# The RG-LRU is computed as a whole beside its gate products; small reciprocal roots become a power on GpSimd

## The chip, the cores and the metric

The kernel runs on one NeuronCore of a Trainium2 chip. The number that counts is the device time of one execution in microseconds (us). Beside it stands one profiled execution, whose span runs from its first to its last instruction.

## The reference

Two layers of a diffusion backbone run over 256 context tokens and 512 latent tokens (T = 768 columns), with a model width of 1024. In each layer one input projection feeds three branches, each 512 channels wide: differential attention, a bidirectional gated recurrence (RG-LRU) and a bidirectional gated DeltaNet. Their outputs are merged by gates, projected and followed by an MLP. The branch that is changed is this, cut to its core:

```python
r = sigmoid(x @ gate_w[d, 0] + gate_b[d, 0])       # per direction d, x after a width-4 convolution
i = sigmoid(x @ gate_w[d, 1] + gate_b[d, 1])
log_a = -LRU_C * r * softplus(-lam[d])
a = exp(log_a)
b = sqrt(-expm1(2 * log_a)) * (i * x)
h_t = a_t * h_(t-1) + b_t                          # context first, then latent; d = 1 backwards
out = gelu(y) * (h of d=0 + h of d=1)
```

The reciprocal roots belong to the RMS norms and the l2 norms, `rsqrt(mean(x*x) + EPS)`. The second layer computes no context outputs, so there most of the work is 512 columns wide, while keys, values and the states of both recurrences still need the context.

## The kernel before, in words

**Matrix products.** Each fp32 product is made of three products of rounded parts. A weight unit `raw` (512 KB) is loaded by SP's DMA queue, ScalarE rounds it to `wh` and VectorE makes the rest `wl` (`split`, L176). The pools `raw`, `wts` (`wh`) and `wtl` (`wl`) hold three units each. `mm_feat` (L203) multiplies: for each of 8 input blocks `wh` with the high part, `wh` with the low part, `wl` with the high part.

**Recurrence and fill.** `gdn_core` ends in a recurrence of 24 steps (`pgd` tiles, L725 to L829), each step a chain TensorE, ScalarE, TensorE, VectorE, TensorE, ScalarE. Behind it in the program stand the "fill" projections, which do not need its result: gates of the merge (`fill_gate`, `pgt`), the RG-LRU's input (`fill_lx`, `plx`) and its gate products (`fill_lx_gates`, `plg`), the gelu input (`fill_ly`, `py`), the DeltaNet's output gate (`fill_gz`, `pz`), queries, keys and values (`pqk`, `pv`). A scheduler orders all instructions when the program is built. It takes the ready instruction that stands first in the program, except inside `tc.high_priority()`, which moves evictions and weight loads ahead. So the fill goes into the recurrence's gaps. Once built, each engine runs its own list strictly in order.

**Buffers.** An instruction that first writes a tile is ready only if the pool has a free buffer. Two pools matter here: `t3` (six buffers of 776 columns) holds nearly all intermediate tiles of the fill, and `big` holds two PSUM tiles, which every fill product needs one of. A PSUM tile is free again when ScalarE has evicted it into a `t3` tile. One `t3` buffer is held by the tile `rope` of `da_tables` (L1047): its second use (L1055, L1058, for the queries' tables) writes tiles with the tags `gcol` and `geb`, and these buffers belong to `R.col` and `R.ge`, which the recurrence reads to its last step.

**RG-LRU.** It has 4 channel blocks j and 2 directions d. Inside the fill, `fill_lx_gates` makes the four gate products of a block, evicts each as `lsg` (L924) and stores it to DRAM (`lrs`). After the recurrence `lru` (L1003 to L1031) loads them into `slab` tiles (`lW`) and does the rest: Exp, Tanh and Square on ScalarE, a VectorE product, Sqrt, products with the gated input, three scans on VectorE, a sum on GpSimd and the product with the stored gelu value `lys`. It runs at the same time as `gdn_out` and the attention's key preparation (`da_load`, `da_keys`, with `dkx` and `pdt`). On ScalarE, Sqrt and the pair Exp/Tanh need different function tables (ACT_TABLE_LOAD).

**Small roots.** `rsqrt` (L130) is called 23 times on 128 x 2 to 128 x 48 values: Sqrt on ScalarE, reciprocal and a Newton step on VectorE.

Of the kernel before, what the change touches and what calls it, by code (L numbers as in the profile page):

```python
# [48 lines left out]
def hybrid_prefix_dit_block_kernel(  # L49
# [68 lines left out]
    epsc = cp.tile([P, 1], F32, name="epsc")  # L118
    G.memset(epsc, EPS)
# [118 lines left out]
    lrs = [dp.tile([P, 4, T], F32, name=f"lrs{i}") for i in range(4)]  # L238
# [192 lines left out]
    def norm(xT, L, gcol, sh, sc, name, parts, sq):  # L431
# [5 lines left out]
        for v, o, m in parts:  # L437
            nt = m // P
            with tc.high_priority():
# [6 lines left out]
                rsqrt(r6[:, 0:nt], v6[:, 0:nt], nt, ps[:, 0:nt], 1.0 / D)  # L446
# [460 lines left out]
    def fill_lx_gates(l, L, j, y, weights):  # L907
# [3 lines left out]
        for a0, a1, o, src in parts:  # L911
            S.copy(yh[:, a0:a1], src)
            G.tensor_tensor(yl[:, a0:a1], src, yh[:, a0:a1].bitcast(F32), op=OP.subtract)
        for d in range(2):
            for g in range(2):
                ps = big("plg")
                i = 2 * d + g
                for n, (w, x) in enumerate(((wh, yh), (wh, yl), (wl, yh))):
# [78 lines left out]
    def lru(l, L, full, mark):  # L997
        last = [None]
        t0 = 0 if full else TC
        lh = slab("lh").rearrange("p (k t) -> p k t", k=4)  # L1000

        def act(*args, **kw):
            i = S.activation(*args, **kw)  # L1003
            if last[0] is not None:
                behind(i, last[0])
            last[0] = i

        for j in range(4):
            W = []
# [492 lines left out]
```

## Time and profile before

| | |
|---|---|
| median of 3 runs | 2781.7 us (2779.94 to 2784.17) |
| profiled execution, its own time | 2784.37 us |
| its span | 2782.6 us |
| TensorE busy | 2652.2 us, 95% of the span |
| VectorE, ScalarE, GpSimd busy | 54%, 40%, 18% |
| mean granted TensorE clock | 0.973 |

Busy times are sums over the instructions of an engine. TensorE instructions are pipelined and their ends are modelled, so a TensorE that is shown busy can still be slowed by its clock: 1.00 is 2.4 GHz, 0.50 is 1.2 GHz, and values between them are means over a stretch. What a stage costs is read from that stage.

### The profile page before, as it was taken

The page shows a single profiled execution, that of the slowest core. Times are in us where ns is not written, and L with a number is a line of the kernel's source. Part 1 is how long each engine was busy: PE and PEld are TensorE (multiplying, and loading weights), DVE is VectorE, ACT ScalarE, POOL GpSimd, SP SyncE. Part 2 cuts the span into 40 slices and gives each one's busy share as a digit, 9 for nine tenths or more (in the row PEclk, how much of TensorE's full clock was granted, in tenths as well). Part 3 has the DMA queues.
Part 4 walks back from the last instruction along what each step waited for, and adds up shares of the span by engine and source line. Part 5 has one row for each costly group of instructions (what it writes and reads, how often), then busy time and mean ns, then how long its engine had stood idle before and what let it go on. Part 6 is the DMA issues. An engine that isn't in the chain of part 4 may idle for free. (4 is left out here: it accounts for less than half of the span.)

```text
span 2782.6 us, 44426 instructions
## 1 busy us (share of the span) xinstructions
PE 2652.2 (95%) x17741; PEld 2261.6 (81%) x17741; DVE 1496.1 (54%) x2520; ACT 1105.4 (40%) x2042; POOL 487.6 (18%) x638
## 2 busy tenths in 40 slices
PE   8999999998999989999999989999998698999999
PEld 5788888987888777888888887887997587888887
DVE  6658553557376543333333476786437776544344
ACT  4242454357366233221222243345437655432321
POOL 3001221214112122110101120032222311211100
PEclk9989999998999999999999999999999699999999
DMA  8433232245433643333332222334225343333332
GB/s 274 138 88 94 83 104 99 78 145 160 150 99 101 205 132 114 121 104 118 121 114 76 85 76 75 105 111 145 81 70 180 138 125 103 99 105 97 93 99 76
DMA packets 315589, 318.67 MB, mean 115 GB/s; under 512 B 19500, under 2 KB 268408, under 8 KB 314488
## 3 DMA queue, kind: packets, MB, share of 16 engines
q1 hardware_dynamic: 315384, 315.84, 36.1%
q8 instruction: 140, 2.29, 0.4%
q14 instruction: 65, 0.53, 0.1%
HBM read 259.70 MB, written 56.10 MB: 113 GB/s over the span
## 5 line engine op out<-in xcount | busy, mean ns | idle before, releaser
L176 ACT CAST wh<-raw 128x1024 fp32r<-128x1024 f32 x288 | 302.2, 1049 | 935.4 <-PE pm L203 614.1
L176 DVE TENSOR_TENSOR wl<-raw,wh 128x1024 fp32r<-128x1024 f32 x288 | 365.0, 1267 | 450.0 <-ACT wh L176 441.1
L203 PE MATMUL pm<-hdh,wh 128*128 128x256 f32 (+1 forms) x896 | 297.4, 332 | 0.5
L203 PE MATMUL pm<-hdl,wh 128*128 128x256 f32 (+1 forms) x896 | 294.5, 329 | 0.0
L203 PE MATMUL pm<-hdh,wl 128*128 128x256 f32 (+1 forms) x896 | 294.3, 328 | 0.0
L1325 DVE SCALAR_TENSOR_TENSOR xT<-pm,mod,xT 128x256 f32<-128x256 f32 (+1 forms) x224 | 133.8, 597 | 235.8 <-PE pm L203 235.8
L203 PE MATMUL pm<-hml,wh 128*128 128x512 f32 (+1 forms) x800 | 243.7, 354 | 5.8 <-DVE hml L461 5.8
L203 PE MATMUL pm<-hmh,wh 128*128 128x512 f32 (+1 forms) x800 | 242.4, 352 | 4.1 <-ACT mr L1306 2.8
L203 PE MATMUL pm<-hmh,wl 128*128 128x512 f32 (+1 forms) x800 | 240.3, 349 | 0.0
L1308 POOL TENSOR_TENSOR mq<-mr 128x768 f32<-128x768 f32 (+1 forms) x64 | 106.5, 1664 | 692.6 <-ACT mr L1306 684.3
L203 PEld LDWEIGHTS pm<-hdh,wh 128*128 128x128 f32 x896 | 170.1, 190 | 30.2 <-DVE xT L1325 8.4
L203 PE MATMUL pgt<-hnh,wh 128*128 128x512 f32 x576 | 181.0, 368 | 10.4 <-ACT gty L873 10.4
L203 PEld LDWEIGHTS pm<-hdh,wl 128*128 128x128 f32 x896 | 170.1, 190 | 15.2
L203 PEld LDWEIGHTS pm<-hdl,wh 128*128 128x128 f32 x896 | 170.2, 190 | 14.7
L203 PE MATMUL pgt<-hnh,wl 128*128 128x512 f32 x576 | 181.9, 365 | 0.0
L203 PE MATMUL pgt<-hnl,wh 128*128 128x512 f32 x576 | 178.1, 364 | 0.0
L203 PEld LDWEIGHTS pm<-hmh,wh 128*128 128x128 f32 x800 | 134.5, 190 | 32.4 <-ACT mr L1306 6.5
L203 PEld LDWEIGHTS pm<-hml,wh 128*128 128x128 f32 x800 | 135.4, 190 | 25.8 <-DVE hml L461 6.7
L203 PEld LDWEIGHTS pm<-hmh,wl 128*128 128x128 f32 x800 | 136.0, 191 | 21.7
L203 PEld LDWEIGHTS pgt<-hnh,wh 128*128 128x128 f32 x576 | 98.4, 194 | 27.7 <-ACT gty L873 12.0
L203 PEld LDWEIGHTS pgt<-hnh,wl 128*128 128x128 f32 x576 | 98.4, 193 | 16.8
L203 PEld LDWEIGHTS pgt<-hnl,wh 128*128 128x128 f32 x576 | 98.2, 195 | 16.7
(431 smaller groups left out, 6058.4 us busy)
## 6 DMA issues: line engine op xcount, KB each, us to landing
raw<-in_mlp_w_dram SPq DMA_DIRECT2D x128, 512.0 KB, 4.0
raw<-in_w_in_dram SPq DMA_DIRECT2D x120, 512.0 KB, 4.1
raw<-in_ada_w_dram SPq DMA_DIRECT2D x80, 512.0 KB, 4.2
lrs<-lsg SPq DMA_DIRECT2D x32, 384.0 KB, 2.3
lW<-lrs SPq DMA_DIRECT2D x16, 768.0 KB, 4.7
raw<-in_w_branch_dram SPq DMA_DIRECT2D x24, 512.0 KB, 3.9
gts<-gty SPq DMA_DIRECT2D x24, 384.0 KB, 4.8
mgg<-gts SPq DMA_DIRECT2D x24, 384.0 KB, 4.2
```

What stands on the lines that cost most here:

```text
L176: return S.copy(hi, src), V.tensor_tensor(lo, src, hi.bitcast(F32), op=OP.subtract)
L203: last = PE.matmul(ps[:, o:o + n], lhsT=w, rhs=r[:, t0:t0 + n], start=(k == 0 and i == 0), stop=(k == nk - 1 and i == 2))
L1308: G.tensor_tensor(q[:, 0:nt], r[:, 0:nt], r[:, 0:nt], op=OP.mult)
L1325: V.scalar_tensor_tensor(xv, ps[:, 0:m], L.mod[:, 40 + n, v:v + 1], xv, op0=OP.mult, op1=OP.add)
```

## The change

`fill_lx_gates` and the long `lru` are gone. `fill_lru` takes their place in the fill: all of the RG-LRU of a block is done from its gate products to the sum of both directions, in `t3` tiles, with no store or load between. Its tiles are the input `ly`, per direction the gate `lsg` that becomes the root, the decay `lat`, the square `lu`, and a second `lsg` (the input gate, which becomes h). `fill_ly` follows it and multiplies the gelu value with that sum; one result is stored per block (`lys`), and `lru` only loads it. The blocks now run as lx, gz, lru, ly each. `rsqrt` has no Sqrt and no reciprocal: GpSimd raises the value to the power -0.5.

```diff
-    def rsqrt(dst, v, n, src=None, scale=1.0):
-
-        w = mp.tile([P, 3, 48], F32, name="rsq", tag="rsq")
-        s, r, u = (w[:, i, 0:n] for i in range(3))
-        if src is None:
-            S.activation(s, v, AF.Sqrt)
-        else:
-            S.activation(s, src, AF.Sqrt, scale=scale, bias=epsc)
-        V.reciprocal(r, s)
+    def rsqrt(dst, v, n):
+
+        w = mp.tile([P, 2, 48], F32, name="rsq", tag="rsq")
+        r, u = (w[:, i, 0:n] for i in range(2))
+        G.tensor_tensor(r, v, bc(mhalf, [P, n]), op=OP.pow)
         V.scalar_tensor_tensor(u, r, -0.5, r, op0=OP.mult, op1=OP.mult)
...
-    def fill_lx_gates(l, L, j, y, weights):
+    def fill_lru(l, L, full, j, y, weights):
+
+        t0 = 0 if full else TC
         wh, wl = weights
         yh, yl = (gp.tile([P, T], F32R, name="gy", tag="g") for _ in range(2))
         parts = ((0, TC, 512, y[:, 0:TC]), (TC, T, 0, y[:, 259:771]))
         for a0, a1, o, src in parts:
             S.copy(yh[:, a0:a1], src)
             G.tensor_tensor(yl[:, a0:a1], src, yh[:, a0:a1].bitcast(F32), op=OP.subtract)
+
+        def gate(i):
+            ps = big("plg")
+            for n, (w, x) in enumerate(((wh, yh), (wh, yl), (wl, yh))):
+                for a0, a1, o, src in parts:
+                    PE.matmul(ps[:, o:o + a1 - a0], lhsT=w[:, i, :], rhs=x[:, a0:a1], start=(n == 0), stop=(n == 2))
+            r = t3("lsg")[:, 0:T]
+            for a0, a1, o, src in parts:
+                with tc.high_priority():
+                    S.activation(r[:, a0:a1], ps[:, o:o + a1 - a0], AF.Tanh, scale=0.5,
+                                 bias=L.gb[:, 4 * i + j:4 * i + j + 1])
+            return r
+
+        decay, root = [], []
         for d in range(2):
-            for g in range(2):
-                ps = big("plg")
-                i = 2 * d + g
-                for n, (w, x) in enumerate(((wh, yh), (wh, yl), (wl, yh))):
-                    for a0, a1, o, src in parts:
-                        PE.matmul(ps[:, o:o + a1 - a0], lhsT=w[:, i, :], rhs=x[:, a0:a1], start=(n == 0), stop=(n == 2))
-                r = t3("lsg")
-                for a0, a1, o, src in parts:
-                    with tc.high_priority():
-                        S.activation(r[:, a0:a1], ps[:, o:o + a1 - a0], AF.Tanh, scale=0.5,
-                                     bias=L.gb[:, 8 * d + 4 * g + j:8 * d + 4 * g + j + 1])
-                    if g == 1:
-                        V.scalar_tensor_tensor(r[:, a0:a1], r[:, a0:a1], 1.0, src, op0=OP.add, op1=OP.mult)
-                nc.sync.dma_start(lrs[j][:, 2 * d + g, :], r[:, 0:T])
-
-    def fill_ly(l, L, a, full, j):
+            r = gate(2 * d)
+            at, u = t3("lat")[:, 0:T], t3("lu")[:, 0:T]
+            c = slice(4 * d + j, 4 * d + j + 1)
+            S.activation(at, r, AF.Exp, scale=L.s8[:, c], bias=L.s8[:, c])
+            S.activation(r, r, AF.Tanh, scale=L.ns8[:, c], bias=L.ns8[:, c])
+            S.activation(u, at, AF.Square)
+            V.scalar_tensor_tensor(r, u, 1.0, r, op0=OP.add, op1=OP.mult)
+            decay.append(at)
+            root.append(r)
+        i = S.activation(root[0], root[0], AF.Sqrt)
+        behind(S.activation(root[1], root[1], AF.Sqrt), i)
+        hs = []
+        for d, (at, r) in enumerate(zip(decay, root)):
+            h = gate(2 * d + 1)
+            for a0, a1, o, src in parts:
+                V.scalar_tensor_tensor(h[:, a0:a1], h[:, a0:a1], 1.0, src, op0=OP.add, op1=OP.mult)
+            (V if d else G).tensor_tensor(r, r, h, op=OP.mult)
+            if d == 0:
+                V.tensor_tensor_scan(h, at, r, 0.0, op0=OP.mult, op1=OP.add)
+            else:
+                V.tensor_tensor_scan(h[:, TC - 1::-1], at[:, TC - 1::-1], r[:, TC - 1::-1], 0.0, op0=OP.mult, op1=OP.add)
+                V.tensor_tensor_scan(h[:, T - 1:TC - 1:-1], at[:, T - 1:TC - 1:-1], r[:, T - 1:TC - 1:-1], h[:, 0:1],
+                                     op0=OP.mult, op1=OP.add)
+            hs.append(h)
+        G.tensor_tensor(hs[0][:, t0:T], hs[0][:, t0:T], hs[1][:, t0:T], op=OP.add)
+        return hs[0]
+
+    def fill_ly(l, L, a, full, j, hs):
...
+        V.scalar_tensor_tensor(y[:, 0:nt], y[:, 0:nt], 0.25, hs[:, t0:T], op0=OP.mult, op1=OP.mult)
...
-        last = [None]
+    def lru(full, mark):
         t0 = 0 if full else TC
         lh = slab("lh").rearrange("p (k t) -> p k t", k=4)
-
-        def act(*args, **kw):
-            i = S.activation(*args, **kw)
-            if last[0] is not None:
-                behind(i, last[0])
-            last[0] = i
-
         for j in range(4):
-            W = []
-            for d in range(2):
-                W.append(slab("lW").rearrange("p (k t) -> p k t", k=4))
-                after(nc.sync.dma_start(W[d][:, 0:2, :], lrs[j][:, 2 * d:2 * d + 2, :]), mark)
-            r, ix, at, u = ([W[d][:, i, :] for d in range(2)] for i in range(4))
-            for d in range(2):
-                c = slice(4 * d + j, 4 * d + j + 1)
-                act(at[d], r[d], AF.Exp, scale=L.s8[:, c], bias=L.s8[:, c])
-                act(r[d], r[d], AF.Tanh, scale=L.ns8[:, c], bias=L.ns8[:, c])
-                act(u[d], at[d], AF.Square)
-                V.scalar_tensor_tensor(r[d], u[d], 1.0, r[d], op0=OP.add, op1=OP.mult)
-            for d in range(2):
-                act(r[d], r[d], AF.Sqrt)
-                (V if d else G).tensor_tensor(r[d], r[d], ix[d], op=OP.mult)
-            yl = ix[1]
-            nc.sync.dma_start(yl[:, t0:T], lys[j][:, t0:T])
-            hs, a1, b1, u1 = lh[:, j, :], at[1], r[1], u[1]
-            V.tensor_tensor_scan(hs, at[0], r[0], 0.0, op0=OP.mult, op1=OP.add)
-            V.tensor_tensor_scan(u1[:, TC - 1::-1], a1[:, TC - 1::-1], b1[:, TC - 1::-1], 0.0, op0=OP.mult, op1=OP.add)
-            V.tensor_tensor_scan(u1[:, T - 1:TC - 1:-1], a1[:, T - 1:TC - 1:-1], b1[:, T - 1:TC - 1:-1], u1[:, 0:1],
-                                 op0=OP.mult, op1=OP.add)
-            G.tensor_tensor(hs[:, t0:T], hs[:, t0:T], u1[:, t0:T], op=OP.add)
-            V.scalar_tensor_tensor(hs[:, t0:T], yl[:, t0:T], 0.25, hs[:, t0:T], op0=OP.mult, op1=OP.mult)
+            after(nc.sync.dma_start(lh[:, j, t0:T], lys[j][:, t0:T]), mark)
         return lh
...
-        y = fill_lx(l, L, a, full, 0)
         for j in range(4):
             gw = lx_gate_weights(l, j)
-            fill_ly(l, L, a, full, j)
-            yn = fill_lx(l, L, a, full, j + 1) if j < 3 else None
-            fill_lx_gates(l, L, j, y, gw)
-            y = yn
-        for j in range(4):
+            y = fill_lx(l, L, a, full, j)
             fill_gz(l, L, a, full, j)
+            hs = fill_lru(l, L, full, j, y, gw)
+            fill_ly(l, L, a, full, j, hs)
```

How the built programs stand, at three places. In the changed program the line numbers are shifted by a few: its L785 to L824 is the recurrence, L199 the fill products, L916 the gate products.

First, TensorE in layer 0, from step 4 of the recurrence on. Before: the step's products, then fill rows (`plx`) ahead of the next piece of the chain.

```order
L798 MATMUL pgd<-gB,gW 32x128 x4
L798 MATMUL pgd<-gB,gQT 32x128 x4
L798 MATMUL pgd<-gA,gW 32x128 x4
L798 MATMUL pgd<-gA,gQT 32x128 x4
L760 MATMUL pgd_1936<-gW 128x128 x2
L203 MATMUL plx<-hnl,wh 128x512
L203 MATMUL plx<-hnl,wh 128x256
L203 MATMUL plx<-hnh,wl 128x512
L203 MATMUL plx<-hnh,wl 128x256
L203 MATMUL plx<-hnh,wh 128x512
L203 MATMUL plx<-hnh,wh 128x256
L203 MATMUL plx<-hnl,wh 128x512
```

Now, from the same step on, behind the last row of the fourth gate product of block 0:

```order
L916 MATMUL plg<-gy,gwl 128x512
L793 MATMUL pgd<-gB,gW 32x128 x4
L793 MATMUL pgd<-gB,gQT 32x128 x4
L793 MATMUL pgd<-gA,gW 32x128 x4
L793 MATMUL pgd<-gA,gQT 32x128 x4
L755 MATMUL pgd_1929<-gW 128x128 x2
L813 MATMUL pgd_1929<-gW,gA 128x128
L813 MATMUL pgd<-gW,gA 128x128
L813 MATMUL pgd<-gW,gB 128x128
L813 MATMUL pgd_1929<-gW,gB 128x128
L813 MATMUL pgd<-gW,gA 128x128 x2
L813 MATMUL pgd<-gW,gB 128x128 x2
```

The fill has moved out. Before, 272 pairs of fill products (512 and 256 columns, same weights) and 653 further ones of 256 columns stand between step 4's products and step 23's; now none does. From step 4 to its end the recurrence is 590 rows of `pgd` in one piece, and `py`, the three later blocks, `pqk` and `pv` follow it. In layer 1 it is 578 rows in one piece, from step 2 on; before, 90 such pairs, 168 rows of 512 columns and 720 of 256 stood between step 2's products and step 23's.

Second, ScalarE at the end of the recurrence of layer 0 (L748, L806, L811 are the recurrence's copies; now L743, L801, L806). Before:

```order
L748 COPY gW<-pgd 128x128 x2
L806 COPY gW<-pgd 128x128
L811 ACTIVATE gA<-pgd,gcol 128x128
L806 COPY gW<-pgd 128x128
L811 ACTIVATE gB<-pgd,gcol 128x128
L965 COPY draw<-pqk 128x512
L966 ACTIVATE dsq<-pqk 128x512
L844 ACTIVATE osq<-gO 128x512 x2
L176 CAST wh<-raw 128x1024
L1003 ACTIVATE lW<-lW,s_3986 128x768
```

Now:

```order
L743 COPY gW<-pgd 128x128 x2
L801 COPY gW<-pgd 128x128
L806 ACTIVATE gA<-pgd,gcol 128x128
L801 COPY gW<-pgd 128x128
L806 ACTIVATE gB<-pgd,gcol 128x128
L931 ACTIVATE lu<-lat 128x768
L920 ACTIVATE lsg<-plg,cols 128x256
L920 ACTIVATE lsg<-plg,cols 128x512
L936 ACT_TABLE_LOAD
L936 ACTIVATE lsg<-lsg 128x768
```

The Square of the second direction of block 0 (`lu`) and the eviction of its third gate product stand behind the last step of the recurrence, although their inputs stand some 20 steps ahead of it. The buffers say why: `ly`, two `lsg`, two `lat` and `rope` are six `t3` tiles, and `rope` is let go only at the end of the recurrence. The third and fourth gate product hold both `big` tiles meanwhile.

Third, ScalarE within a block after the recurrence (block 1 of layer 0), against the gate evictions of a block before. Before:

```order
L924 ACTIVATE lsg<-plg,cols 128x256
L924 ACTIVATE lsg<-plg,cols 128x512
L912 CAST gy<-ly 128x256
L912 CAST gy<-ly 128x512
L729 ACTIVATE gW<-gVt,gcol 128x128 x2
L731 ACTIVATE gW<-gKt,gcol 128x128
L748 COPY gW<-pgd 128x128 x2
L731 ACTIVATE gW<-gKt,gcol 128x128
L176 CAST gwh<-gw 128x512
L937 COPY lyy<-py 128x768
L938 ACTIVATE lyq<-py 128x768
```

Now:

```order
L929 ACTIVATE lat<-lsg,s_3979 128x768
L930 ACTIVATE lsg<-lsg,ns_3980 128x768
L931 ACTIVATE lu<-lat 128x768
L920 ACTIVATE lsg<-plg,cols 128x256
L920 ACTIVATE lsg<-plg,cols 128x512
L929 ACTIVATE lat<-lsg,s_3979 128x768
L935 ACT_TABLE_LOAD
L935 ACTIVATE lsg<-lsg 128x768
L172 CAST wh<-raw 128x1024
L930 ACT_TABLE_LOAD
L930 ACTIVATE lsg<-lsg,ns_3980 128x768
L931 ACTIVATE lu<-lat 128x768
```

Between the eviction of the first gate product and that of the third (the first row below this piece) now stand two Exp, two Tanh, two Squares, a Sqrt, two table loads and a weight rounding. On TensorE the order in a block is `plx`, `pz`, 24 rows of `plg`, `py`, then `plx` of the next block.

## Rows read from the trace of the kernel before

**Rows 1.** Busy time by stage: from:to, length, PE, PEld, DVE, ACT, POOL, PEclk, DMA, GB/s.

```profile
328.70:589.30 260.60, 253.97 (x2353) 222.86 (x2341) 128.67 (x312) 114.38 (x292) 65.94 (x123) 0.99 0.31 99
1864.00:2111.80 247.80, 239.68 (x2214) 207.70 (x2216) 126.24 (x310) 111.16 (x293) 60.75 (x121) 0.99 0.30 95
600.00:680.00 80.00, 65.00 (x387) 57.49 (x386) 69.34 (x86) 66.21 (x74) 33.86 (x17) 0.89 0.59 187
2140.00:2240.00 100.00, 74.31 (x294) 60.64 (x293) 72.70 (x76) 70.19 (x94) 28.45 (x18) 0.74 0.46 157
```

**Rows 2.** Waits of PE behind the recurrence of layer 1 (2112 to 2250 us).

```profile
PE pdt L1101 <- DVE dkx L176: 13.7, 9, 6.6
```

**Rows 3.** Timeline of ACT: first copy (L806) of some steps of the recurrence.

```profile
328.70 0.27 ACT L806 COPY gW<-pgd 128x128 f32<-128x128 f32 x1 [2.23 <-PE pgd L798]
...
589.26 0.27 ACT L806 COPY gW<-pgd 128x128 f32<-128x128 f32 x1 [3.16 <-PE pgd L798]
...
1864.01 0.47 ACT L806 COPY gW<-pgd 128x128 f32<-128x128 f32 x2
...
2092.90 0.27 ACT L806 COPY gW<-pgd 128x128 f32<-128x128 f32 x1 [1.77 <-PE pgd L798]
...
2106.33 0.27 ACT L806 COPY gW<-pgd 128x128 f32<-128x128 f32 x1 [0.46 <-PE pgd L798]
...
2111.81 0.27 ACT L806 COPY gW<-pgd 128x128 f32<-128x128 f32 x1 [0.82 <-PE pgd L798]
```

**Rows 4.** Timeline of PE: fill products of 256 columns, and of 512 and 256 in pairs.

```profile
2065.67 0.28 PE L220 MATMUL pqk<-wh,hnh 128*128 128x256 f32 x1
...
2067.47 0.28 PE L220 MATMUL pqk<-wh,hnh 128*128 128x256 f32 x1
...
232.44 0.53 PE L203 MATMUL pgt<-hnh,wh 128*128 128x512 f32 x2
...
235.62 0.53 PE L203 MATMUL pgt<-hnh,wh 128*128 128x512 f32 x2
```

**Rows 5.** The tile `rope`: its readers on DVE.

```profile
L1058 DVE TENSOR_TENSOR das<-rope,dag x8: 283/292/549, 299.2 to 2110.5; 128x128 f32<-128x128 f32 x8
```

**Rows 6.** ACT by line: count, busy us, mean ns, idle before and releasers.

```profile
L176 ACT CAST wh<-raw 128x1024 fp32r<-128x1024 f32 x288 | 302.2, 1049 | 935.4 <-PE pm L203 614.1 <-PE pgt L203 97.0 <-PE pop L203 41.0
...
L924 ACT ACTIVATE lsg<-plg,cols 128x256 f32<-128x256 f32 x64 | 33.4, 589 | 14.4 <-DMA lrs<-lsg 6.9 <-PE pgd L760 2.6 <-PE plg L920 2.0
...
L1003 ACT ACT_TABLE_LOAD x22 | 28.2, 1283 | 0.4
L1003 ACT ACTIVATE lW<-lW 128x768 f32<-128x768 f32 x32 | 26.7, 837 | 4.6 <-DVE lW L1019 4.5
...
L1003 ACT ACTIVATE lW<-lW,s 128x768 f32<-128x768 f32 x16 | 16.4, 1024 | 2.2 <-DMA lW<-lrs 2.1
...
L884 ACT ACTIVATE zz<-pz,cols 128x768 f32<-128x768 f32 (+1 forms) x8 | 6.3, 788 | 0.0
```

**Rows 7.** The tile `lW` (the RG-LRU before): min/median/max ns.

```profile
L1019 DVE SCALAR_TENSOR_TENSOR lW<-lW x16: 923/957/2174, 606.2 to 2175.7; 128x768 f32<-128x768 f32 x16
L1022 POOL TENSOR_TENSOR lW<-lW x8: 1804/1854/2777, 615.0 to 2182.6; 128x768 f32<-128x768 f32 x8
L1026 DVE TENSOR_TENSOR_SCAN lh<-lW x8: 1725/1745/3379, 618.6 to 2189.2; 128x768 f32<-128x768 f32 x8
```

**Rows 8.** The page: VectorE's part of a weight split.

```profile
L176 DVE TENSOR_TENSOR wl<-raw,wh 128x1024 fp32r<-128x1024 f32 x288 | 365.0, 1267 | 450.0 <-ACT wh L176 441.1
```

**Rows 9.** Two stretches by stage (columns as in Rows 1): recurrence alone, and attention.

```profile
2099.00:2102.00 3.00, 3.00 (x38) 2.31 (x32) 0.76 (x3) 1.07 (x4) 0.55 (x2) 0.51 0.00 0
...
2106.00:2112.00 6.00, 5.29 (x88) 4.00 (x76) 4.52 (x18) 1.60 (x8) 0.91 (x2) 1.00 0.01 3
...
2196.00:2214.00 18.00, 16.46 (x58) 13.95 (x59) 10.68 (x12) 12.48 (x19) 1.66 (x2) 0.50 0.00 1
```

**Rows 10.** The small roots: ACT's table loads at line L136.

```profile
L136 ACT ACT_TABLE_LOAD  x11: 1283/1283/1283, 13.7 to 2332.9; - x11
```

More of the change, by code (lines that the diff above doesn't have):

```diff
@@ L117, in hybrid_prefix_dit_block_kernel @@
     V.tensor_tensor(fold, ident[:, 0:64], ident[:, 64:128], op=OP.add)
-    epsc = cp.tile([P, 1], F32, name="epsc")
-    G.memset(epsc, EPS)
+    mhalf = cp.tile([P, 1], F32, name="mhalf")
+    G.memset(mhalf, -0.5)
     bdm = cp.tile([P, HEADS, 32], F32, name="bdm")
@@ L237, in hybrid_prefix_dit_block_kernel @@
     dqs = [dp.tile([P, 6, 512], F32, name=f"dqs{i}") for i in range(2)]
-    lrs = [dp.tile([P, 4, T], F32, name=f"lrs{i}") for i in range(4)]
     mss = [dp.tile([P, T], F32, name=f"mss{i}") for i in range(8)]
@@ L445, in norm @@
                 V.tensor_scalar(v6[:, 0:nt], ps[:, 0:nt], 1.0 / D, EPS, op0=OP.mult, op1=OP.add)
-                rsqrt(r6[:, 0:nt], v6[:, 0:nt], nt, ps[:, 0:nt], 1.0 / D)
+                rsqrt(r6[:, 0:nt], v6[:, 0:nt], nt)
                 rb[o] = spread(r6, nt)
@@ L995, in lru_tables @@
         V.tensor_scalar(L.s8, L.s8, -4.0, None, op0=OP.mult)
-    def lru(l, L, full, mark):
-        last = [None]
+    def lru(full, mark):
         t0 = 0 if full else TC
         lh = slab("lh").rearrange("p (k t) -> p k t", k=4)
-        def act(*args, **kw):
-            i = S.activation(*args, **kw)
-            if last[0] is not None:
-                behind(i, last[0])
-            last[0] = i
-        for j in range(4):
-            W = []
-            for d in range(2):
-                W.append(slab("lW").rearrange("p (k t) -> p k t", k=4))
-                after(nc.sync.dma_start(W[d][:, 0:2, :], lrs[j][:, 2 * d:2 * d + 2, :]), mark)
-            r, ix, at, u = ([W[d][:, i, :] for d in range(2)] for i in range(4))
-            for d in range(2):
-                c = slice(4 * d + j, 4 * d + j + 1)
-                act(at[d], r[d], AF.Exp, scale=L.s8[:, c], bias=L.s8[:, c])
-                act(r[d], r[d], AF.Tanh, scale=L.ns8[:, c], bias=L.ns8[:, c])
-                act(u[d], at[d], AF.Square)
-                V.scalar_tensor_tensor(r[d], u[d], 1.0, r[d], op0=OP.add, op1=OP.mult)
-            for d in range(2):
-                act(r[d], r[d], AF.Sqrt)
-                (V if d else G).tensor_tensor(r[d], r[d], ix[d], op=OP.mult)
-            yl = ix[1]
-            nc.sync.dma_start(yl[:, t0:T], lys[j][:, t0:T])
-            hs, a1, b1, u1 = lh[:, j, :], at[1], r[1], u[1]
-            V.tensor_tensor_scan(hs, at[0], r[0], 0.0, op0=OP.mult, op1=OP.add)
-            V.tensor_tensor_scan(u1[:, TC - 1::-1], a1[:, TC - 1::-1], b1[:, TC - 1::-1], 0.0, op0=OP.mult, op1=OP.add)
-            V.tensor_tensor_scan(u1[:, T - 1:TC - 1:-1], a1[:, T - 1:TC - 1:-1], b1[:, T - 1:TC - 1:-1], u1[:, 0:1],
-                                 op0=OP.mult, op1=OP.add)
-            G.tensor_tensor(hs[:, t0:T], hs[:, t0:T], u1[:, t0:T], op=OP.add)
-            V.scalar_tensor_tensor(hs[:, t0:T], yl[:, t0:T], 0.25, hs[:, t0:T], op0=OP.mult, op1=OP.mult)
+        for j in range(4):
+            after(nc.sync.dma_start(lh[:, j, t0:T], lys[j][:, t0:T]), mark)
         return lh
@@ L1427, in hybrid_prefix_dit_block_kernel @@
             if o == "L":
-                lh = lru(l, L, full, R.end)
+                lh = lru(full, R.end)
             if o == "D":
```

## The prediction

> **What bounds the kernel now.** The stages first [rows 1]: TensorE is busy nearly everywhere, so time can be won only where it waits or runs at the lower clock. Two such places touch this change: the 80 us behind the recurrence of layer 0, with 65.0 us busy, and the 100 us behind that of layer 1, with 74.3 us busy at a mean clock of 0.74. Their idle time is 15.0 + 25.7 = 40.7 us. The wait named there is the key transposes `pdt` on VectorE's `dkx`, 13.7 us in nine times [rows 2], while VectorE and ScalarE are 70% busy and more [rows 1]. A part of that work is the RG-LRU. The recurrence looks harmless: in layer 0 TensorE is busy 254.0 of 260.6 us at clock 0.99.
>
> What keeps it busy there is the fill. Products of 256 columns follow each other every (2067.47 - 2065.67) / 15 = 0.120 us, pairs of 512 and 256 every (235.62 - 232.44) / 9 = 0.353 us [rows 4], so one of 512 takes 0.353 - 0.120 = 0.233 us. Between step 4 and step 23 of layer 0, 589.26 - 328.70 = 260.6 us apart [rows 3], the printed order has 272 pairs and 653 products of 256: 96.0 + 78.4 = 174.4 us. The rest, 86.2 us over 19 steps, is what a step costs beside fill: 4.54 us. In layer 1, step 2 to 23, 2111.81 - 1864.01 = 247.8 us [rows 3], the fill is 90 pairs, 168 of 512 and 720 of 256: 31.8 + 39.1 + 86.4 = 157.3 us. That leaves 90.5 us over 21 steps, 4.31 us each.
>
> **What the change does, part by part.** The printed order decides it. The RG-LRU does not run inside the recurrence. Block 0 fills the six `t3` buffers with `ly`, two `lsg`, two `lat` and `rope`; the last reading of `rope` is at 2110.5 us in layer 1, at the last steps [rows 5], and the orders of both programs have it there in both layers. So `lu` waits for the end of the recurrence, two gate products wait in PSUM for it, and all other fill waits for PSUM behind them on TensorE's queue. This costs twice.
>
> First, the bare recurrence. The trace has three bare steps, at the end of layer 1: (2111.81 - 2092.90) / 3 = 6.30 us, the last of them 5.48 us [rows 3]. The first two contain other ScalarE work and 3 us at the lower clock level, 1.2 GHz [rows 9]; I take 5.9 us, midway. Layer 0: 19 x 5.9 = 112.1 us for 86.2, **+25.9**. In layer 1 six steps have context alone and no query products; I estimate 5.2 us from the same row: 15 x 5.9 + 6 x 5.2 = 119.7 us for 90.5, **+29.2**. The fill itself is paid behind the recurrence at the rate at which it was paid inside.
>
> Second, the RG-LRU of each block now stands between TensorE's products. In a block `py` comes behind all four gate products in the queue and needs one of the two PSUM tiles that the third and fourth hold. The third is evicted when ScalarE has worked off its list: two `pz` evictions (2 x 0.79), first gate (2 x 0.59), Exp 1.02, Tanh (taken like the Exp) 1.02, Square 0.84, second gate 1.18, Exp 1.02, table load 1.28, Sqrt 0.84, weight rounding 1.05, table load 1.28, Tanh 1.02, Square 0.84, then VectorE's product 0.96, which frees `lu`, then the eviction 1.18 [rows 6, 7]. That is 16.3 us from the end of `pz`; TensorE has 24 gate products (12 pairs, 4.2 us) in it, so 12.1 us are idle. Then `py` runs, and `plx` of the next block needs its `wl`, which stands in VectorE's list behind the scans: two products 0.96 each, GpSimd's product 1.85, scan 1.75, eviction 1.18, product 0.96, backward scans (taken as one of 768 columns) 1.75, `wl` 1.27 [rows 6 to 8], 10.7 us. `py` covers 24 x 0.353 = 8.5 us of it in layer 0 and 24 x 0.233 = 5.6 us in layer 1; 2.2 and 5.1 us are idle. The clock will be at the lower level for some us after such a pause, but `py` is what then runs, and what it loses lies in that second wait. So a block costs 14.3 us in layer 0 and 17.2 us in layer 1, for three blocks. Block 0 has only its end left: Square, product and eviction, 3.0 us, and the second wait. Layer 0: 42.9 + 5.2 = **48.1 us**; layer 1: 51.6 + 8.1 = **59.7 us**.
>
> The Trainium skill ("ScalarE: Activation LUTs", What ACT_TABLE_LOAD costs) has a table switch at 1.28 us and as much again of draining, 2.66 us. The trace does not agree on the second half: 22 table loads of 1283 ns have 0.4 us of idle time before them in all [rows 6]. By the page two loads on each of six paths would add 2 x 1.38 x 6 = 16.5 us; I leave it out.
>
> What is won: the RG-LRU is gone from behind the recurrence, with its stores and loads (no wait of TensorE named them). `gdn_out` has the fill beside it now, and the key tiles stand between gate products in the new order. Lower bound 0, if the key preparation waits as long without the RG-LRU; upper bound the idle 40.7 us plus what the lower clock took, at most 65.0 x 0.11 + 74.3 x 0.26 = 26.5 us [rows 1], 67 us. I take **-40.7**: some idle time stays in layer 1, where 28 key transposes stand without fill, and some clock comes back.
>
> The small roots: 23 powers on GpSimd, an operation that no row shows. Away go a short ScalarE and VectorE instruction each and 11 table loads of 1.28 us [rows 10]. About 12 of the calls are waited for. If a power is as cheap as a trivial instruction, the gain is at most the 11 loads, 14 us; if it is as dear as GpSimd's product of 128 x 768, 1.85 us [rows 7], the loss is 12 x 1.85 less some loads, about 10 us. I take 0 and keep -14 to +10.
>
> **The sum**, against the profiled execution's own 2784.4 us: 25.9 + 29.2 + 48.1 + 59.7 - 40.7 = +122.2, 2906.6 us. That execution lies 2.7 us above the median, so **2904 us**.
>
> **The rivals.**
> *The lower clock holds in the bare recurrence.* In attention TensorE stayed at 0.50 for 18 us though shown 91% busy [rows 9], and a bare step has pauses. But 2106 to 2112 us, bare as well, ran at 1.00. There TensorE is shown busy 5.29 of 6 us [rows 9]: if all of that lay on the step's path, half the clock would stretch 5.48 us by 88% to 10.3 us, if none, by nothing. Midway, 7.9 us a step, the addition is (19 + 21) x 2.0 = +80, **2984 us**. The Trainium skill ("TensorE: Matmul & The Clock Gate", A second HAM failure mode) tells of a matmul kernel whose short pauses between groups make the clock swing again and again. The trace bears that out for the 3 us at 0.51, not for the steps around it.
>
> *Milder stalls.* Steps at 5.48 us (-17), a chain a quarter shorter because ScalarE's instructions overlap and the weight rounding slips out of it (-27), and the transition won wholly with its clock (-18): **2842 us**.
>
> *Faster after all.* The one mechanism is that TensorE does not wait in the blocks: if the third gate is evicted before the ScalarE list is through, because a `t3` buffer is free earlier than I read it, the 48.1 + 59.7 us fall away and the gain behind the recurrence is left against the bare steps: 2904 - 108 = 2796 us, and with milder bare steps and the whole transition 2796 - 17 - 18 = **2761 us**. It decides once the stall per block falls under some 2 us. Against it: the list is strictly in order, and the eviction is printed behind the second Square.
>
> *The bare recurrence hides.* The change would be neutral if in the end only the fill moved: +55.1 for the bare steps against -40.7 and milder stalls; it needs the same mechanism.
>
> **How the numbers follow.** Likeliest, stalls as summed: 0.62, its own range 2865 to 2950 (step 5.5 to 6.3 us, chain 20% either way). Lower clock: 0.15. Milder: 0.17. Faster or neutral: 0.06. The range holds the likeliest and the milder case and reaches towards the lower clock, half of whose weight it takes in: 2835 to 2985 us. 0.2% (5.6 us) is about what a measurement of this kernel can tell from no change; by these cases: faster 0.04, same 0.02, slower 0.94.
>
> **What the profile will show if this holds.** Two stretches of some 115 to 125 us in which TensorE has only `pgd`, steps 5.5 to 6.3 us apart (at 8 us the clock rival is right). Behind each, three times per layer, a pause of TensorE before `py` of about 10 us, named as waiting for ScalarE's `lsg`, and a shorter one before or in `plx` waiting for `wl`. Behind the recurrence the `pdt` waits fall to a few us. The small roots cost no visible wait. It would be wrong if fill stood between the `pgd` steps in the trace, if `py` followed the gates at once, or if GpSimd's power took many us and held the norms up.

## The result: 4.5% slower

| | before | after |
|---|---|---|
| median | 2782.9 us (4 runs, 2779.94 to 2785.44) | 2906.9 us (4 runs, 2904.53 to 2910.75) |
| span of the profiled execution | 2782.6 us | 2902.8 us |
| ratio | | 1.0447, 95% interval 1.0429 to 1.0465 |

The forecast was 2904 us (2835 to 2985). The spans of the two profiled executions differ by 120.2 us; the sum of the prediction was 122.2.

The stages of the changed kernel (columns as in [rows 1]): for each layer the recurrence without fill, up to the first copy of its last step; the fill behind it up to the first product of queries and keys; the rest up to the attention's score products.

```profile
331.02:451.53 120.51, 99.79 (x1128) 77.44 (x1132) 59.74 (x217) 56.11 (x191) 44.08 (x105) 0.84 0.01 3
455.30:595.30 140.00, 110.25 (x577) 93.68 (x577) 82.78 (x100) 83.48 (x109) 24.11 (x24) 0.86 0.25 79
595.30:820.80 225.50, 222.65 (x1579) 209.45 (x1578) 85.73 (x123) 75.74 (x107) 44.24 (x24) 0.99 0.41 129
1922.75:2046.67 123.92, 100.44 (x1154) 77.56 (x1158) 59.87 (x216) 62.33 (x205) 44.09 (x105) 0.85 0.01 3
2049.50:2184.20 134.70, 96.17 (x401) 76.09 (x401) 75.20 (x95) 80.45 (x109) 25.16 (x24) 0.82 0.23 70
2184.20:2433.70 249.50, 240.93 (x1600) 220.42 (x1599) 141.26 (x215) 118.08 (x227) 51.74 (x30) 0.97 0.40 128
```

The kernel before, from the end of its recurrence to the score products of layer 0 (the first) and of layer 1 (the last), which ends the third and sixth row above too:

```profile
593.70:764.30 170.60, 152.91 (x922) 135.72 (x921) 102.68 (x131) 104.89 (x128) 42.92 (x25) 0.93 0.50 164
2114.70:2317.20 202.50, 172.49 (x895) 147.17 (x894) 153.22 (x213) 143.87 (x245) 46.01 (x30) 0.87 0.46 152
```

The recurrence now takes 120.5 and 123.9 us from the same steps at which [rows 3] begin, against 260.6 and 247.8 with fill. The fill of those stretches (174.4 and 157.3 us by the prediction's count) is paid behind it. The blocks' products are worth 276 pairs of 0.353 = 97.4 us in layer 0, and 108 pairs and 168 products of 0.233 = 77.3 us in layer 1. So the pieces of the sum can be read one by one:

| term | predicted | measured |
|---|---|---|
| bare recurrence, layer 0 | +25.9 | 120.5 - 86.2 = +34.3 |
| bare recurrence, layer 1 | +29.2 | 123.9 - 90.5 = +33.4 |
| blocks behind it, layer 0 | +48.1 | 140.0 - 97.4 = +42.6 |
| blocks behind it, layer 1 | +59.7 | 134.7 - 77.3 = +57.4 |
| transition behind the recurrence | -40.7 | (225.5 + 97.4 - 174.4 - 170.6) + (249.5 + 77.3 - 157.3 - 202.5) = -22.1 - 33.0 = -55.1 |
| all else | 0 | 120.2 - 112.6 = +7.6 |

What TensorE waits for, over the whole changed kernel (us in total, times, longest); the key transposes `pdt` waited 25.6 us for `dkx` in the whole kernel before (13.7 of them in [rows 2]) and are down to 3.5:

```profile
PE py L199 <- ACT lsg L920: 37.0, 8, 7.0
PE pgd L793 <- ACT gW L743: 21.1, 32, 1.7
PE plg L916 <- ACT lsg L920: 15.5, 9, 2.5
...
PE plg L916 <- ACT gy L909: 5.3, 3, 2.3
...
PE pdt L1095 <- DVE dkx L172: 3.5, 3, 2.3
```

One block, the second of layer 0, on ScalarE (start, length, tile; in brackets idle time before it and its releaser):

```profile
485.09 0.80 ACT L878 ACTIVATE zth<-pz 128x768 f32<-128x768 f32 x1
485.80 0.89 ACT L879 ACTIVATE zz<-pz,cols 128x768 f32<-128x768 f32 x1
486.95 1.05 ACT L920 ACTIVATE lsg<-plg,cols 128x256 f32<-128x256 f32 x2 [0.27 <-PE plg L916]
...
492.88 1.28 ACT L935 ACT_TABLE_LOAD   x1
494.18 0.84 ACT L935 ACTIVATE lsg<-lsg 128x768 f32<-128x768 f32 x1
494.92 1.03 ACT L172 CAST wh<-raw 128x1024 fp32r<-128x1024 f32 x1
495.97 1.28 ACT L930 ACT_TABLE_LOAD   x1
497.26 1.03 ACT L930 ACTIVATE lsg<-lsg,ns 128x768 f32<-128x768 f32 x1
498.20 0.83 ACT L931 ACTIVATE lu<-lat 128x768 f32<-128x768 f32 x1
500.05 1.05 ACT L920 ACTIVATE lsg<-plg,cols 128x256 f32<-128x256 f32 x2 [1.03 <-DVE lsg L932]
```

The same moments on TensorE, and on VectorE the `wl` that the next `plx` needs:

```profile
491.85 1.65 PE L916 MATMUL plg<-gy,gwh 128*128 128x256 f32 x4 [2.46 <-ACT lsg L920]
501.16 1.01 PE L199 MATMUL py<-hnh,wh 128*128 128x512 f32 x2 [7.01 <-ACT lsg L920]
...
495.98 1.23 DVE L172 TENSOR_TENSOR wl<-raw,wh 128x1024 fp32r<-128x1024 f32 x1 [4.13 <-ACT wh L172]
```

In this block the chain is the one that was foreseen, instruction by instruction: from the first `pz` eviction (485.1) to `py` (501.2) 16.1 us, predicted 16.3. In the other two blocks of layer 0 it takes 14.8 and 16.2 us. What was not foreseen is the last row: `wl` stands ahead of the scans, so the second wait of a block does not exist.

In layer 1 the chain is longer, 19.6, 19.3 and 21.0 us. There `pz` has only 512 columns, and ScalarE must still round the gates' input `gy` behind its eviction; TensorE waits for that, and ScalarE then for TensorE. The second block of layer 1, ScalarE and then TensorE:

```profile
2072.96 0.59 ACT L878 ACTIVATE zth<-pz 128x512 f32<-128x512 f32 x1
2078.32 1.06 ACT L920 ACTIVATE lsg<-plg,cols 128x256 f32<-128x256 f32 x2 [2.84 <-PE plg L916]
...
2075.01 1.87 PE L916 MATMUL plg<-gy,gwh 128*128 128x256 f32 x6 [1.12 <-ACT gy L909]
2092.52 0.79 PE L199 MATMUL py<-hnh,wh 128*128 128x512 f32 x1 [7.01 <-ACT lsg L920]
```

### The profile page after: what moved, and what is told of

Same layout as the page of the kernel before. It is cut to its first block, busy times and chain, and to the rows that moved or that the text cites. A ratio compares the mean times of both kernels' runs of the same rounds, so it can differ in the third digit from the quotient of the medians.

```text
span 2902.8 us, 44325 instructions
## 1 busy us (share of the span) xinstructions
PE 2698.5 (93%) x17741; PEld 2299.9 (79%) x17741; DVE 1481.0 (51%) x2497; ACT 1095.4 (38%) x2006; POOL 536.8 (18%) x661
## 5 line engine op out<-in xcount | busy, mean ns | idle before, releaser
L199 PE MATMUL pm<-hdh,wh 128*128 128x256 f32 (+1 forms) x896 | 297.4, 332 | 0.5
L199 PE MATMUL pm<-hdl,wh 128*128 128x256 f32 (+1 forms) x896 | 294.5, 329 | 0.0
L199 PE MATMUL pm<-hdh,wl 128*128 128x256 f32 (+1 forms) x896 | 294.2, 328 | 0.0
L199 PE MATMUL pm<-hml,wh 128*128 128x512 f32 (+1 forms) x800 | 244.3, 354 | 5.0 <-DVE hml L456 5.0
L199 PE MATMUL pm<-hmh,wh 128*128 128x512 f32 (+1 forms) x800 | 243.3, 353 | 4.0 <-ACT mr L1300 2.8
L199 PE MATMUL pm<-hmh,wl 128*128 128x512 f32 (+1 forms) x800 | 241.1, 350 | 0.0
L199 PEld LDWEIGHTS pm<-hdh,wh 128*128 128x128 f32 x896 | 170.1, 190 | 30.1 <-DVE xT L1319 7.5
L199 PEld LDWEIGHTS pm<-hdh,wl 128*128 128x128 f32 x896 | 170.1, 190 | 15.3
L199 PEld LDWEIGHTS pm<-hdl,wh 128*128 128x128 f32 x896 | 170.2, 190 | 14.8
L199 PE MATMUL pgt<-hnl,wh 128*128 128x512 f32 x576 | 177.0, 358 | 0.0
L199 PE MATMUL pgt<-hnh,wl 128*128 128x512 f32 x576 | 175.4, 357 | 0.0
L199 PE MATMUL pgt<-hnh,wh 128*128 128x512 f32 x576 | 174.9, 357 | 0.0
L199 PEld LDWEIGHTS pm<-hmh,wh 128*128 128x128 f32 x800 | 135.4, 191 | 32.1 <-ACT wh L172 6.5
L199 PEld LDWEIGHTS pm<-hml,wh 128*128 128x128 f32 x800 | 136.0, 191 | 25.3 <-DVE hml L456 5.9
L199 PEld LDWEIGHTS pm<-hmh,wl 128*128 128x128 f32 x800 | 136.7, 191 | 21.6
L199 PEld LDWEIGHTS pgt<-hnl,wh 128*128 128x128 f32 x576 | 96.3, 189 | 15.4
L199 PEld LDWEIGHTS pgt<-hnh,wh 128*128 128x128 f32 x576 | 95.6, 190 | 15.4
L199 PEld LDWEIGHTS pgt<-hnh,wl 128*128 128x128 f32 x576 | 95.7, 190 | 15.2
```

The source lines that it names most:

```text
L199: last = PE.matmul(ps[:, o:o + n], lhsT=w, rhs=r[:, t0:t0 + n], start=(k == 0 and i == 0), stop=(k == nk - 1 and i == 2))
```

## The experiments

**The buffer that shuts the fill out.** First `da_tables` behind the blocks, so that `rope` asks for a `t3` buffer last:

```diff
-        Q = da_tables(l)
         lru_tables(L)
         for j in range(4):
             ...
             fill_ly(l, L, a, full, j, hs)
+        Q = da_tables(l)
```

> The changed kernel, but `da_tables` (and with it the tile `rope`) stands behind the four RG-LRU blocks in the program, so that the blocks' tiles come to the six `t3` buffers first. Theory A (the buffer that `rope` keeps to the end of the recurrence shuts the fill out): the fill is back between the recurrence's steps, the last step starts about 260 us behind step 4 in layer 0 again, no pause of 7 us before `py` is seen by TensorE because recurrence products run in it, and what was won behind the recurrence stays. 2783 + 8 (small roots) - 40 to 62 (behind the recurrence): 2729 to 2751 us. Theory B (the blocks' ScalarE chain is too long to be covered even inside the recurrence): half of the block stalls stay, some 2790 us. Theory C (the place of `rope` is without effect): 2907 us.

Measured: 2805.1 us, 1.008 of before (1.0065 to 1.0096). Then the same table through a buffer of its own, `da_tables` left in its place:

```diff
-        rp = t3("rope")
-        nc.sync.dma_start(rp[:, 0:512], rope.rearrange("p s t f -> p (s t f)"))
...
+            rc = lp.tile([P, 4, 64], F32, name="rope", tag="rope")
+            nc.sync.dma_start(rc, rope[:, 0])
...
+            rs = lp.tile([P, 4, 64], F32, name="rope", tag="rope")
+            nc.sync.dma_start(rs, rope[:, 1])
...
```

(The edit also makes the keys' tables ahead of the queries'.)

> The changed kernel, `da_tables` where it was, but its table comes in halves of 1 KB through a buffer of its own, so that no `t3` buffer is held. Theory A (it is the held buffer): the same as with `da_tables` behind the blocks, within 6 us. If it was the program order of `da_tables` and not the buffer that shut the fill out: 2907 us still.

Measured: 2811.7 us (1.0105, 1.0088 to 1.0121). Two different ways of freeing the sixth buffer bring 102 and 95 us back, so the buffer it was. The second loads the table at the very start, where VectorE waits 9.6 us for it and TensorE then 8.0 us for VectorE's `hnl` (0.6 in the changed kernel), which would make the difference. But theory A was half wrong: the first is still 20 us slower than before, above its 2729 to 2751 us and above theory B's 2790. The stages of the first of them, the recurrence from step 4 of layer 0 and from step 2 of layer 1, and TensorE's main waits:

```profile
337.22:596.28 259.06, 243.68 (x2128) 207.91 (x2131) 156.05 (x339) 143.21 (x317) 83.68 (x134) 0.93 0.21 63
1872.68:2154.77 282.09, 256.61 (x2147) 215.83 (x2151) 160.49 (x343) 157.87 (x344) 81.74 (x133) 0.90 0.19 57
```

```profile
PE pgd L793 <- ACT gW L743: 18.7, 8, 6.0
PE plg L916 <- ACT lsg L920: 11.0, 8, 2.3
```

The fill is back, and TensorE idles 15.4 and 25.5 us in the two recurrences, at a mean clock of 0.93 and 0.90, where it idled 6.6 and 8.1 us at 0.99 [rows 1]. The RG-LRU now stands between the recurrence's copies in ScalarE's list, and one copy kept TensorE waiting 6.0 us.

**The bare recurrence alone.** The kernel before with its fill held back:

```diff
...
+                    if hold[0] is not None and k == 0:
+                        behind(last, hold[0])
...
             fill_ly(l, L, a, full, j)
+            hold[0] = R.turn
             yn = fill_lx(l, L, a, full, j + 1) if j < 3 else None
```

> The kernel before, with the products of the fill from the second input product on held back until the recurrence's last products are issued. This is the bare recurrence alone, without the new RG-LRU between the products. The recurrence without fill costs +68 by the changed kernel's trace (+55 as predicted); behind it the old RG-LRU and the key preparation now have some 190 us of fill beside them, which wins up to 40 (as predicted) or 62 (as the changed kernel's trace reads): 2784 + 68 - 40 to 62 = 2790 to 2812 us. If the RG-LRU between the products was no loss and the bare recurrence all of it: 2890 us or more.

Measured: 2827.6 us (1.0162, 1.0146 to 1.0178), +44.5 us, between the two expectations and in neither. The recurrences take 119.5 and 123.3 us over the steps that take 120.5 and 123.9 in the changed kernel:

```profile
324.61:444.14 119.53, 100.30 (x1136) 78.03 (x1136) 60.21 (x219) 53.80 (x190) 44.44 (x106) 0.84 0.02 6
1888.54:2011.79 123.25, 102.07 (x1156) 79.34 (x1152) 57.84 (x214) 54.01 (x194) 43.51 (x104) 0.81 0.01 2
```

The recurrence without fill is thus not all of the loss. Of the +66 of both layers (33.3 + 32.8) only some 22 us are won back elsewhere, while the old RG-LRU still stands behind it, though with fill beside it. From here to the changed kernel it is another 79 us: the blocks, less what it wins to have the RG-LRU gone from there.

**What a block waits for.** The changed kernel without table switches, which leaves the root out:

```diff
-        i = S.activation(root[0], root[0], AF.Sqrt)
-        behind(S.activation(root[1], root[1], AF.Sqrt), i)
+        i = S.activation(root[0], root[0], AF.Copy)
+        behind(S.activation(root[1], root[1], AF.Copy), i)
```

> The changed kernel with a plain copy in place of the RG-LRU's Sqrt (this leaves the root out), so that ScalarE loads no function table in the blocks. If ScalarE's list is what a block's `py` waits for (the chain of the prediction): two of its table loads, 1.28 us each, stand ahead of the third gate's eviction in each of six blocks, 15 us less, 2892 us (2885 to 2897); the two behind it are covered by `py`. If VectorE's products and scans, or the lower clock behind each pause, set the block's length: within 5 us of 2907.

Measured: 2888.9 us (1.0386, 1.0368 to 1.0404), 18 us less, as ScalarE's list would have it. The wait of `py`, 37.0 us, is down to

```profile
PE py L199 <- ACT lsg L920: 25.2, 8, 5.0
```

Then an order that halves the loads but leaves two of them ahead of the third gate's eviction (`gate` sets its evictions behind the instruction that it is handed):

```diff
-            S.activation(u, at, AF.Square)
+            sq = S.activation(u, at, AF.Square)
...
         i = S.activation(root[0], root[0], AF.Sqrt)
-        behind(S.activation(root[1], root[1], AF.Sqrt), i)
+        behind(i, sq)
+        sq = S.activation(root[1], root[1], AF.Sqrt)
+        behind(sq, i)
...
-            h = gate(2 * d + 1)
+            h = gate(2 * d + 1, sq)
```

> The changed kernel with that order on ScalarE alone (`rope` where it was). If a block waits for the eviction of its third gate, the half of the loads that falls away here gains nothing, since the two that stay stand ahead of that eviction, with one Sqrt more: 6 x 0.84 = 5 us more, 2912 us (2905 to 2916). If the sum of ScalarE's work counts: 20.5 us less in all, half of it in the blocks behind the recurrence: 2893 us (2887 to 2899).

Measured: 2908.7 us (1.0451, 1.0435 to 1.0466): 16 loads less, nothing gained. `py` waits

```profile
PE py L199 <- ACT lsg L920: 44.4, 7, 7.7
```

So it is the place in the list ahead of the third eviction that counts, as the prediction's chain had it, and not ScalarE's sum of work.

**Why it does not win with the fill inside.** The copy in place of the Sqrt (the edit above, which leaves the root out) in the kernel with `da_tables` behind the blocks:

> The changed kernel with `da_tables` behind the blocks, and again a copy in place of the RG-LRU's Sqrt (the root is left out). There the RG-LRU stands in ScalarE's list between the recurrence's copies, and TensorE waited 33 us for these copies and for gate evictions. If ScalarE's time is what the recurrence waits for, the 32 table loads (41 us of ScalarE) count: 2805 - 15 to 25 = 2780 to 2790 us. If it is the order of the lists and not their length, or the clock alone: 2805 us, within 6.

Measured: 2785.2 us (1.0014, 1.0003 to 1.0025), 20 us less. ScalarE's time does count inside the recurrence, and even with all 32 loads gone the moved RG-LRU does not beat the kernel before (+2 us). The order with half of the loads, in the same kernel:

> The changed kernel with `da_tables` behind the blocks, and with an order on ScalarE: both Sqrt behind the second Square, and the evictions of the third and fourth gate behind the second Sqrt. A block then has two table loads in place of four, 16 less in all, 20.5 us of ScalarE. Without the 32 loads it was 20 us faster; half of them: 2805 - 10 = 2795 us (2789 to 2800). If the later eviction of the third gate costs as much (it holds a PSUM tile longer): 2805 us or more.

Measured: 2806.5 us (1.0083, 1.007 to 1.0096), no change. The waits for the copies fall, and one that was not there takes their place:

```profile
PE py L199 <- ACT lsg L920: 12.0, 8, 2.2
PE pgd L793 <- ACT gW L743: 11.0, 7, 4.6
```

That order with the blocks spread over the recurrence and the table in its own buffer:

```diff
             fill_ly(l, L, a, full, j, hs)
+            if j == 0:
+                Q = da_tables(l, R.first)
+            if j < 2:
+                fill_qk(l, L, a, full, Q, 1, j)
+            else:
+                fill_v(l, L, a, full, j - 2)
...
```

> That order on ScalarE, the rope table through a 1 KB buffer of its own (loaded behind the first step of the recurrence), and the fill in another order: keys behind block 0 and block 1, values behind block 2 and block 3, so that the four RG-LRU blocks lie spread over the recurrence. If the RG-LRU's ScalarE work, crowded into the first half of the recurrence, is what still costs there (waits for the recurrence's copies, and the lower clock behind them): those 20 to 30 us come back too, 2775 us (2762 to 2788), faster than both. If a block's own chain is what costs, wherever it lies: 2795 us, as without the spreading.

Measured: 2812.1 us (1.0104, 1.0088 to 1.012). So spreading the blocks out is no cure: `py` still waits 9.5 us for gates and the recurrence 20.0 us for its copies. That it came out above both numbers is not explained; three things were changed at once.

**The transition.** The kernel before with keys ahead of the RG-LRU:

```diff
-        for o in "kvqGLD":
+        for o in "kvqGDL":
```

> The kernel before, with one pair of letters exchanged: the attention's key preparation stands ahead of the old RG-LRU in the program. The term of what was won behind the recurrence, tested alone: if the keys waited because all four blocks of the RG-LRU stand ahead of them in VectorE's and ScalarE's lists, most of the idle 40.7 us and some of the clock come back at no other cost, 2739 to 2764 us. If the wait only moves (the RG-LRU is then late for the merge, or the keys wait for their own load and powers): 2784 us, within 6.

Measured: 2836.6 us (1.0194, 1.018 to 1.0208), slower by 53 us, which neither theory had. TensorE uses its gate products up beside the keys, and then has nothing beside the RG-LRU. The main waits (`pmf` is the merge), and a stage of layer 0:

```profile
PE pmf L203 <- ACT brh L176: 59.3, 4, 22.3
PE pdt L1101 <- DVE dqh L1132: 17.1, 7, 4.3
```

```profile
740.00:765.00 25.00, 2.75 (x11) 2.21 (x10) 17.76 (x19) 22.36 (x27) 8.31 (x4) 0.50 0.49 151
```

And the split, two blocks ahead of each half of the keys (`lru` called with blocks 0 and 1, `da_keys(Q, 0)`, `lru` with 2 and 3, `da_keys(Q, 1)`):

> The kernel before, with the old RG-LRU split around the first half of the key preparation: blocks 0 and 1, keys of the first half, blocks 2 and 3, keys of the second half. With all blocks ahead of the keys TensorE waited 25.6 us for `dkx`, with all behind them 59 us for the merge. If the two waits are one shortage (ScalarE and VectorE have more work there than TensorE has products beside it), the split only shares it out: 2784 to 2800 us. If the keys of the first half are enough to keep TensorE busy: 2765 us (2755 to 2775), faster than before.

Measured: 2780.5 us (0.9988, 0.9979 to 0.9997), 3 us less, just below the range for a shortage that is only shared out and far from the 2765 us; `pdt` still waits 16.6 us on ScalarE's `dkx` and 13.8 us on VectorE's. In both orders tried the wait only moves. What won the transition in the changed kernel was the RG-LRU's leaving it.

**The small roots.** The kernel before with the new `rsqrt`, and the changed kernel with the old one (the lines of the diff in either direction):

> The kernel before with the new small roots alone. By the trace of the changed kernel a power of 128 x 2 takes 0.70 us on GpSimd, one of 128 x 48 takes 8.0 us, and 8 us of the 120 lie in stages that only the roots touch: +8 us, 2791 us (2786 to 2797). If the roots are covered, as the prediction took it: 2783 us, within 3.

Measured: 2782.9 us (0.9998, 0.9987 to 1.0008).

> The changed kernel with the small roots of before (Sqrt, reciprocal). If the roots cost what the stages that only they touch show: 8 us less, 2899 us (2893 to 2904). If they are covered: 2907 us, within 3. If the old roots' table loads cut into the RG-LRU's ScalarE list: over 2907 us.

Measured: 2911.6 us (1.0459, 1.0444 to 1.0475), 4.7 us above the changed kernel's median, with overlapping intervals. The roots are not the +7.6: both expectations that made them so fell, and the prediction's 0 stands. GpSimd does get slower by them, in the changed kernel:

```profile
L135 POOL TENSOR_TENSOR rsq<-v,mhalf x9: 697/708/1333, 15.2 to 2535.7; 128x2 f32<-128x2 f32 x8, 128x6 f32<-128x6 f32 x1
...
L135 POOL TENSOR_TENSOR rsq<-dss,mhalf x4: 5428/8011/8018, 635.9 to 2283.1; 128x48 f32<-128x48 f32 x3, 128x32 f32<-128x32 f32 x1
L135 POOL TENSOR_TENSOR rsq<-dso,mhalf x4: 1646/1646/2907, 912.7 to 2449.4; 128x8 f32<-128x8 f32 x3, 128x16 f32<-128x16 f32 x1
L135 POOL TENSOR_TENSOR rsq<-qv,mhalf x2: 4150/4153/4156, 206.6 to 1829.7; 128x24 f32<-128x24 f32 x2
```

No kernel here with the RG-LRU moved beats the one before.

## Why the prediction was right, and where it was off

**Fill shut out by `rope`: right, shown.** Freeing that buffer alone, in two ways, brings the fill back and 95 to 102 us.

**Bare recurrence: right in kind, 12.6 us too small** (67.7 for 55.1). The step was taken as 5.9 us; it is 6.34 in layer 0 (120.5 / 19) and 5.90 as the mean of all 21 in layer 1 (5.70 predicted). Single steps (columns as in [rows 1]): in layer 0 the first one, one at full clock, and two near the end; then the first of layer 1:

```profile
331.02:339.56 8.54, 5.97 (x48) 4.81 (x52) 3.87 (x11) 5.08 (x13) 2.24 (x5) 0.51 0.07 15
387.35:392.80 5.45, 4.61 (x72) 3.57 (x64) 2.64 (x10) 2.80 (x11) 2.49 (x6) 1.00 0.00 2
...
427.68:436.83 9.15, 6.00 (x68) 4.63 (x64) 5.69 (x16) 4.97 (x14) 2.51 (x6) 0.69 0.01 2
436.83:444.54 7.71, 7.05 (x68) 5.78 (x64) 3.23 (x12) 2.17 (x8) 0.88 (x2) 0.50 0.00 1
...
1922.75:1933.61 10.86, 7.11 (x46) 5.27 (x46) 4.25 (x10) 10.80 (x19) 2.16 (x5) 0.61 0.01 3
```

The two first steps are 2.6 and 5.7 us above what was taken for them (5.9, and 5.2 with context alone): the step was priced bare, but there ScalarE still works at block 0's RG-LRU between the step's copies, and in layer 0 TensorE waits for two of these copies:

```profile
331.38 1.01 PE L813 MATMUL pgd<-gW,gA 32*128 32x128 f32 x4 [2.68 <-ACT gW L801]
334.18 0.58 PE L813 MATMUL pgd<-gW,gB 32*128 32x128 f32 x2 [1.79 <-ACT gW L801]
```

In the step of 9.15 us other ScalarE and VectorE work (`osq`, `oss`) holds TensorE up for 2.7 us. The other full steps are near the 5.9 that was taken: 6.05 in layer 0 and 5.94 in layer 1 on average, a mixture of steps at full clock (5.45 us), steps at the lower level (7.7 us) and some between. But the kernel before with its fill held back, which has no RG-LRU in its first steps, is no shorter there (119.5 and 123.3 us, mean clock 0.84 and 0.81). So how much of the 12.6 us is that ScalarE work, and how much the lower clock that comes without it too, stays open.

The rival of the lower clock had the price right (7.9 us for a step at the lower level) and the duration wrong: the lower level comes and goes, the mean is 0.84. The Trainium skill ("TensorE: Matmul & The Clock Gate", A second HAM failure mode) tells of a swing between two levels in another kernel, where pauses are short and frequent; this trace agrees, with 1.00 and 0.50 in the steps above.

**Blocks: the sum near (100.0 for 107.8), its parts not.** The chain to `py` was right within 0.2 us in the block shown, and the runs without table loads and with fewer show that it is what `py` waits for. The step that failed is "`plx` of the next block needs its `wl`, which stands in VectorE's list behind the scans": it stands ahead of them, and the 29.2 us of second waits are 0. Most of that is made up for elsewhere. The pause before `py`, foretold as about 10 us, is 7.0 at most, since 2.5 us of the waiting come ahead of the fourth gate product (the row at 491.85). Over the six blocks the chain took 106.9 us where 6 x 16.3 = 97.8 were summed, all of it in layer 1, whose rounding of `gy` the sum left out. And what `py` loses to the clock, which the prediction let lie in the second wait, now shows. TensorE at `py` in the two stages:

```profile
455.30:595.30 140.00, 39.50 (x192) 0.86 0.25 79
2049.50:2184.20 134.70, 29.65 (x96) 0.82 0.23 70
```

That is 69.2 us where 96 pairs of 0.353 and 96 products of 0.233 are worth 56.3, so 12.9 us more. The clock of a pause and of the `py` behind it, in the second block of layer 0:

```profile
485.00:501.00 16.00, 6.17 (x25) 4.13 (x23) 5.86 (x6) 14.55 (x19) 1.53 (x2) 0.70 0.22 66
501.00:510.00 9.00, 8.84 (x40) 7.65 (x41) 4.75 (x6) 4.57 (x6) 1.83 (x1) 0.77 0.01 2
```

In all, the two stages show TensorE idle for 140.0 - 110.25 = 29.8 and 134.7 - 96.17 = 38.5 us, and busy for 31.7 us more than the products are worth. Of these 31.7 us, 7.0 are transposes of `gdn_out` (`pot`), which in the kernel before lie in the stage up to the score products, and are no cost of the blocks. That the lower clock makes the rest is inferred, not shown.

**Transition: 14 us too small** (-55.1 for -40.7, within the bounds 0 to 67). The idle time fell by 36.3 us (from 17.7 + 30.0 to 2.9 + 8.6), 5.6 us are those transposes, which only moved, and the other 13.2 go with a clock of 0.99 and 0.97 in place of 0.93 and 0.87. In the two reordered kernels, which keep the RG-LRU there, the win does not come.

**Small roots: 0, right**, by two kernels. The powers are dearer than the upper bound taken (8.0 us for 48 columns, bound 1.85), but they lie beside other work, with two exceptions: `pdo` waits 4.9 us for `dtok` behind a power at the end of layer 1's attention, in both kernels with powers, where it is 2.0 us in three times without; and in the kernel before with powers `pdt` waits 34.5 us for `dkx`, where it is 25.6 without. Against them stand the table loads that are saved; the time did not change.

**All else, +7.6,** was not in the sum. 3.7 us of it lie behind the last score products (2902.8 - 2433.7 against 2782.6 - 2317.2), 2.3 us ahead of the first stretch (331.0 against 328.7) and 2.3 us between the layers' stages (1922.75 - 820.80 against 1864.00 - 764.30). What makes them is not settled.

The errors of +12.6, -7.8, -14.4 and +7.6 cancel to -2. The mechanisms were confirmed but for the second wait, and that the sum came so close is luck. One price among the rivals does not follow either: the transition "won wholly with its clock" is put at 18 us more, where the prediction's own bound gives up to 26.5.

## What to carry to other kernels

Before moving work into a stage, count the buffers of the pool that it will live in, with those that another tile holds to the end of the stage: one buffer too few shut the whole fill out here and cost 100 us. Work whose result must be evicted by the engine that also does the long elementwise chain stops the matrix engine once all PSUM tiles wait in that chain, and here only what stood ahead of the eviction in that engine's list counted. Before moving elementwise work from a stage that lacks cover into one with cover, see whether the covering chain uses the same engine: here it did, and with the fill back inside the recurrence the move still lost 20 us.

## What the runs showed of the hardware

A power on GpSimd is paid by the column: 0.71 us for 128 x 2, 1.65 for 8, 4.15 for 24, 8.01 for 48, or (8.01 - 4.15) / 24 = 0.16 us for each column, where a product of 768 columns takes 1.85 us [rows 7]. And a TensorE that was shown busy 83% of the time in a chain of small dependent products (99.8 of 120.5 us) did not keep its clock: the mean was 0.84, with whole steps at 1.00 (5.45 us) and at 0.50 (7.71 us) in one stretch.
